# Two feed-forward stages of a two-layer trunk: first weights loaded by SyncE, first product in free PSUM banks, another order of the first 15 block products and of the work beside them

## The chip, the cores and the metric

The kernel runs on one core of a Trainium2 chip. The time is the device time of one execution in microseconds (us), median over several executions; lower is better. Matrix products run on TensorE (PE in the profile), elementwise work on VectorE (DVE), ScalarE (ACT) and GpSimd (POOL); SyncE (SP) issues most transfers. Each engine works through its own queue in order. PSUM, where PE accumulates, has eight banks of 128 x 512 floats.

## The reference

A sequence of 1024 tokens with 1024 features goes through two residual layers (a gated DeltaNet layer, then chunked attention), each followed by the same feed-forward block, and a last RMSNorm. The change touches the feed-forward blocks:

```python
def conv_ffn(xn, w_up, conv_w, conv_b, w_down):
    h = causal_dwconv(xn @ w_up, conv_w) + conv_b
    gate, val = h[..., :FFN_DIM], h[..., FFN_DIM:]
    return (jax.nn.silu(gate) * val) @ w_down
...
h = h + conv_ffn(rmsnorm(h, f_norm[layer]), f_w_up[layer], f_conv[layer], f_conv_b[layer], f_w_down[layer])
```

FFN_DIM is 2816, which is 22 tiles of 128 channels, once for `gate` and once for `val`. The convolution has three taps along the sequence. All is float32.

## The kernel before, in words

**Products.** Every float32 product is made of three matmuls on rounded operands: a value is cut into a high part (a cast to `fp32r`, mostly on ACT) and a low part (the value minus its high part, on POOL or DVE), and `triple` (lines 1394 to 1397) adds high x high, high x low of the moving operand, and low of the weights x high. A block product has four such triples, so 12 matmuls of 128 x 512. In the profile the weights' parts are called uh and ul (ring "u"), dh and dl (ring "d"), and those of the hidden channels eh and el. The activations' parts are xh and xl.

**The feed-forward stage** is one function, `ffn`, called once per layer (layer 0 at line 1974, layer 1 at line 2484; their PE work begins at 674 us and 1896 us). The up-projection of channel tile 0 is done plainly, in eight block products: two halves of the sequence, gate and val, two halves of the 1024 input features. The tiles 1 to 20 use a seven-product (Strassen-like) scheme: product (j, n) is number n of tile j. It needs sums of blocks of the normed activations (`sums`, `highs`, `lows` for n = 7, 6, 5, 4: four 128 x 512 pieces each) and of the weights (`left_sum`), and its results are put together in `after`: product 1 is copied from PSUM to `keep` by ACT, and product 2 is then added into the same PSUM bank; product 4 is added into the bank of product 7, product 3 into that of product 5. From the finished gate and val of a tile come the three taps each (`taps`: step 0 on ACT, steps 1 and 2 on DVE), `silu` on ACT and the product `gated` on DVE. The down-projection takes pairs of tiles, again by seven products (`second(g, n)`, tiles `pd`), whose PSUM results `drain` copies or adds into `stage`.

**The order is written by hand.** `step` appends one PE block to the list `seq`; I number the blocks of a layer from 0. Blocks 0 to 7 are tile 0. From 8 on come the products, before the change (1,1), (2,1), (1,2), (2,2), (1,7), (1,6), (1,5), (2,7), (1,4), (1,3), (2,6), (2,5), (2,4), (3,1), (2,3), so block 14 is (1,5), 17 is (1,3), 18 is (2,6), 19 is (2,5), 20 is (2,4). Then (3,7) is block 23, and from 24 the `second` blocks of the first pair are interleaved; before the change `second(0,5)` is block 29, (3,4) is 30, `second(0,3)` is 31, (3,3) is 32, (4,1) is 33, `second(0,6)` is 34. `at(i, f, rank)` has the other engines' work `f` put into their queues just before block i, lower ranks first. All this lies in a manual schedule, so each engine's queue has exactly this order.

Operands of a product are made two blocks ahead (lines 1608 to 1616): `left_sum` on DVE, the high part on ACT, the low part on DVE for the blocks before (1,3) and on POOL after.

**The norm in front.** `norm_steps` is a generator that is driven from outside: squares and their sum, `pss` (eight tiny matmuls at L374), root and reciprocal, `psb` (eight small matmuls at L387 that spread the factors), then for each of the eight feature tiles k the scaling (L394, DVE), the high part (L395, ACT) and the low part (L383, DVE or POOL). The second half of the sequence is normed while tile 0's first blocks run: `plain` advances the generator at two places, written as (block, triple), in layer 0 (0, 3) for `pss` and (1, 1) for the rest, in layer 1 (1, 3) and (2, 2). Its last steps on the first half in layer 1 are driven by `tail` (line 2419) in the attention stage.

**Transfers and rooms.** `load` (line 1438) brings 128 x 512 weights. For tile 0 of layer 0 it is issued by POOL, otherwise by SP. `cut0` makes tile 0's operands; for the gate (r = 0) casts and low parts are both on POOL.

**PSUM.** In `ffn` the tag "u" has four one-bank tiles and the tag "d" two two-bank tiles. The tag that is used first gets banks 0 to 3, so "u" does (`pu0` at line 1573). In front of layer 0 the accumulators of the last stage (`acco`) sit in the pool's first three banks; in front of layer 1 they are in the last three, since `pB` is opened before `paccB` (lines 2426, 2427).

## Time and profile before

| | |
|---|---|
| median of 3 runs | 2573.83 us (2572.54 to 2575.7) |
| the profiled execution | 2573.15 us, span of its instructions 2571.4 us |
| PE busy | 2506.2 us, 97% of the span |
| DVE busy | 1824.8 us, 71% |
| ACT busy | 1405.4 us, 55% |
| POOL busy | 1484.8 us, 58% |

A row of the timeline gives the start and the length in us, the engine, the line, the operation, the output and the inputs, shapes, and a count of rows put together; in square brackets is the idle time of that engine before it and what ended it. A row of the windows view gives a stretch, its length, each engine's busy time in it with the count of instructions, and at the end the granted clock of PE (1.00 is full), the share of DMA time and GB/s.

### The profile page before, as it was taken

Reading aid. Unit: us, or ns where it says so; the run is one execution under the profiler, and the core shown is the slowest. Engines: PE = TensorE matmul, PEld = TensorE weight load, DVE = VectorE, ACT = ScalarE, POOL = GpSimd, SP = SyncE. Lnnn points to the kernel's source line nnn. Section 1 sums busy time; section 2 is a strip of 40 time slices with the busy share of each in tenths; the row PEclk is TensorE's granted clock in tenths of the full one; section 3 lists DMA queues with packets and bytes.
Section 4 is the critical chain, followed back from the end, with each engine's and each line's share of the span. In section 5 each row is a group of like instructions: output and inputs, shape, how many; then the busy total and the mean of one; then the engine's idle time right before and its main releaser. Section 6 shows DMA issues by size and latency. Waiting matters only on the chain. (4 is left out here: it accounts for less than half of the span.)

```text
span 2571.4 us, 39303 instructions
## 1 busy us (share of the span) xinstructions
PE 2506.2 (97%) x13957; PEld 2081.7 (81%) x13957; DVE 1824.8 (71%) x2956; ACT 1405.4 (55%) x2704; POOL 1484.8 (58%) x1511
## 2 busy tenths in 40 slices
PE   7999999999999999999999999999999999999998
PEld 5878788888777888888788888888877788888877
DVE  5765775454588888888866666666478788888885
ACT  6444555474456555565545555556455656555653
POOL 3655554245537777777725444445453777777770
PEclk9999999999999999999999999999999999999999
DMA  4534445455326676777841211122332467677785
GB/s 128 138 101 121 119 117 164 130 176 167 112 78 136 143 152 143 155 152 152 185 164 46 61 43 48 53 69 71 128 119 78 135 148 147 146 155 153 155 194 189
DMA packets 317061, 325.93 MB, mean 127 GB/s; under 512 B 32832, under 2 KB 240960, under 8 KB 316864
## 3 DMA queue, kind: packets, MB, share of 16 engines
q1 hardware_dynamic: 285728, 219.33, 28.7%
q0 software_dynamic: 26240, 95.43, 20.7%
q10 hardware_dynamic: 4896, 8.65, 1.0%
q8 instruction: 110, 1.80, 0.3%
q14 instruction: 87, 0.71, 0.1%
HBM read 180.68 MB, written 142.67 MB: 126 GB/s over the span
## 5 line engine op out<-in xcount | busy, mean ns | idle before, releaser
L1362 POOL TENSOR_TENSOR ul<-r,uh 128x512 fp32r<-128x512 f32 x276 | 438.3, 1607 | 276.1 <-ACT uh L1383 261.6
L105 POOL TENSOR_TENSOR wlo<-wraw,whi 128x256 fp32r<-128x256 f32 (+3 forms) x338 | 249.3, 768 | 227.1 <-ACT whi L103 192.4
L120 PE MATMUL acc<-xh,whi 128*128 128x512 f32 x896 | 377.8, 422 | 0.2
L122 PE MATMUL acc<-xh,wlo 128*128 128x512 f32 x896 | 354.9, 396 | 3.2 <-POOL wlo L105 3.2
L121 PE MATMUL acc<-xl,whi 128*128 128x512 f32 x896 | 355.1, 396 | 1.0 <-DVE xl L1102 0.6
L1383 ACT CAST uh<-r 128x512 fp32r<-128x512 f32 x290 | 178.2, 623 | 202.0 <-DVE r L1362 159.0
L1397 PE MATMUL pu<-xh,ul 128*128 128x512 f32 x528 | 207.1, 392 | 3.7 <-POOL ul L1362 3.7
L1395 PE MATMUL pu<-xh,uh 128*128 128x512 f32 x528 | 207.0, 392 | 2.9 <-POOL uh L1383 1.4
L1396 PE MATMUL pu<-xl,uh 128*128 128x512 f32 x528 | 206.5, 391 | 1.0 <-POOL xl L383 1.0
L122 PEld LDWEIGHTS acc<-xh,wlo 128*128 128x128 f32 x896 | 169.7, 189 | 41.4 <-POOL wlo L105 3.9
L1749 ACT COPY stage<-pd 128x1024 f32<-128x1024 f32 x180 | 174.9, 1013 | 50.3 <-PE pd L1397 49.4
L121 PEld LDWEIGHTS acc<-xl,whi 128*128 128x128 f32 x896 | 170.8, 191 | 27.3 <-DVE xl L1102 2.7
L120 PEld LDWEIGHTS acc<-xh,whi 128*128 128x128 f32 x896 | 170.7, 190 | 24.6 <-ACT xh L1101 1.1
L1490 DVE SCALAR_TENSOR_TENSOR gate<-gpre,colt,gate 128x1023 f32<-128x1023 f32 (+2 forms) x92 | 180.0, 1957 | 4.7 <-ACT gate L1487 3.8
L1362 POOL TENSOR_TENSOR dl<-a,dh 128x512 fp32r<-128x512 f32 x90 | 153.8, 1709 | 46.0 <-ACT dh L1383 46.0
L2155 POOL TENSOR_SCALAR sS<-sS,st 128x640 f32<-128x640 f32 (+4 forms) x128 | 85.7, 674 | 163.5 <-DVE st L2153 147.9
L1490 DVE SCALAR_TENSOR_TENSOR val<-vpre,colt,val 128x1023 f32<-128x1023 f32 x88 | 151.9, 1726 | 35.7 <-ACT val L1487 35.5
L2145 DVE CUSTOM_DVE_ANT_0 sS<-sc,bt 128x640 f32<-128x640 f32 (+4 forms) x128 | 84.1, 657 | 123.6 <-PE sc L2141 97.0
L1362 DVE TENSOR_TENSOR r<-r,r 128x512 f32<-128x512 f32 x160 | 126.4, 790 | 31.0 <-POOL ul L1362 29.6
L1397 PEld LDWEIGHTS pu<-xh,ul 128*128 128x128 f32 x528 | 99.5, 188 | 26.7 <-POOL ul L1362 6.2
L2213 ACT CAST pTh<-ptp 128x512 fp32r<-128x512 f32 (+2 forms) x176 | 76.1, 452 | 81.2 <-PE ptp L2200 79.6
L1395 PEld LDWEIGHTS pu<-xh,uh 128*128 128x128 f32 x528 | 99.4, 188 | 24.2 <-POOL uh L1383 1.9
(406 smaller groups left out, 7131.9 us busy)
## 6 DMA issues: line engine op xcount, KB each, us to landing
r<-in_f_w_up_dram SPq DMA_DIRECT2D x172, 256.0 KB, 4.3
d_r<-stage POOLq DMA_DIRECT2D x78, 512.0 KB, 7.7
d_c<-stage POOLq DMA_DIRECT2D x70, 512.0 KB, 7.8
a<-in_f_w_down_dram SPq DMA_DIRECT2D x72, 256.0 KB, 2.8
wraw<-in_a_w_in_dram SPq DMA_DIRECT2D x32, 512.0 KB, 4.7
d_e<-stage POOLq DMA_DIRECT2D x32, 512.0 KB, 8.8
wraw<-in_a_w_out_dram SPq DMA_DIRECT2D x16, 512.0 KB, 4.3
d_r<-h ACTq DMA_DIRECT2D x32, 256.0 KB, 3.4
```

The lines of the kernel that those rows point to most:

```text
L105: nc.gpsimd.tensor_tensor(lo[:, c], raw[:, c], hi[:, c].bitcast(F32), op=ALU.subtract)
L120: mm(ps, hi[:, kw, wcol : wcol + P], rh[k][s], start=st, stop=False)
L121: mm(ps, hi[:, kw, wcol : wcol + P], rl[k][s], start=False, stop=False)
L122: mm(ps, lo[:, kw, wcol : wcol + P], rh[k][s], start=False, stop=sp)
L1362: tt = lambda eng, o, a, b, op: eng.tensor_tensor(o, a, b, op=op)
L1383: copy(hi, src)
L1395: mm(ps, w[0][:, cw], x[0], start=first, stop=False, skip_group_check=True)
L1396: mm(ps, w[0][:, cw], x[1], start=False, stop=False, skip_group_check=True)
L1397: mm(ps, w[1][:, cw], x[0], start=False, stop=last, skip_group_check=True)
L1490: nc.vector.scalar_tensor_tensor(t_[:, a:c1], p_[:, a - step : c1 - step], w[:, 2 - step : 3 - step], t_[:, a:c1], op0=ALU.mult, op1=ALU.add)
L1749: nc.scalar.copy(t_, ps)
L2155: nc.gpsimd.tensor_scalar(S, S, st[:, 3:4], 1.0, op0=ALU.mult, op1=ALU.mult)
```

## The change

- `load`: tile 0 of layer 0 is loaded by SP as all others are.
- PSUM: two unused "d" tiles are taken first, so that "d" has banks 0 to 3 and "u" banks 4 to 7; ahead of layer 1 `paccB` is opened before `pB`, so that there too the accumulators are in the first banks.
- `cut0(0, 0)` is now inside the manual schedule at block 0, rank -1. In layer 1 the norm's last step of the first half (the low part of k = 7) is held back and comes right behind it.
- The norm's second beat in layer 1 is at (2, 0) instead of (2, 2). The low part of k = 6 of the second half goes to POOL.
- The order of the first 15 products; `second(0, 3)` one product later; (3,7) gets its low part on DVE; and the places of taps, silus and products `gated` of tiles 0 to 2, and of `after(1, 2)`.

```diff
         def low(t_, k):
-            eng = (nc.gpsimd if k < 4 else nc.vector) if keep and s == 1 else (nc.vector if k % 2 == 0 else nc.gpsimd)
+            eng = (nc.gpsimd if k in (0, 1, 2, 3, 6) else nc.vector) if keep and s == 1 else (nc.vector if k % 2 == 0 else nc.gpsimd)
...
+        H = {'x': {('s', 7): (5, 1), ('h', 7): (6, 1.5), ('s', 6): (6, 2), ('h', 6): (6, 2.01), ('l', 7): (7, 2), ('l', 6): (8, 2), ('s', 5): (9, 2), ('h', 5): (9, 2.01), ('l', 5): (10, 2.002), ('s', 4): (11, 2), ('h', 4): (11, 2.01), ('l', 4): (12, 2)}, 'xl': {7: (), 6: (), 5: (), 4: ()}, 'beats': ({(0, 3): 1, (1, 1): 20}, {(1, 3): 1, (2, 0): 20}), 'first': [(1, 1), (1, 2), (2, 1), (1, 7), (2, 2), (1, 6), (1, 5), (2, 7), (1, 4), (1, 3), (2, 6), (2, 5), (2, 4), (2, 3), (3, 1)], 'o': (2, 3, 5, 7, 8, 9, 11), 'ops': {(3, 7): (0.5, 1.5, 'v')}, 'conv': {0: {'g0': (11, 0), 'v0': (12, 0), 'v1': (13, 2), 'v2': (13, 2.611), 'g1': (15, 2), 'g2': (15, 2.01), 's': (15, 2.204), 'm': (17, 2)}, 1: {'v0': (18, 2), 'v1': (18, 3.206), 'v2': (19, 2), 'g0': (19, 2.01), 'g1': (20, 2), 'g2': (21, 0.903), 's': (22, 1.6), 'm': (23, 1.3)}, 2: {'v0': (24, 2), 'v1': (24, 2.01), 'v2': (25, 2), 'g0': (26, 1.466), 'g1': (26, 2), 'g2': (27, 2), 's': (28, 1.6), 'm': (29, 1.3)}}, 'gp': {1: (18, 0.411), 2: (22, 3)}}
...
-            (nc.gpsimd if j + layer == 0 else nc.sync).dma_start(out=t_, in_=w_up[k0 * P : (k0 + 4) * P, m * P : (m + 1) * P].rearrange("(k p) m -> p k m", p=P))
+            nc.sync.dma_start(out=t_, in_=w_up[k0 * P : (k0 + 4) * P, m * P : (m + 1) * P].rearrange("(k p) m -> p k m", p=P))
...
         first_ps = {}
+        for _ in range(2):
+            pacc.tile([P, SEQ], F32, name="pu1", tag="d", bufs=2)
...
-                    if (i, k) == ((0, 3), (1, 3))[layer]:
-                        next(tail)
-                    if (i, k) == ((1, 1), (2, 2))[layer]:
-                        for _ in tail:
-                            pass
+                    for _ in range(H["beats"][layer].get((i, k), 0)):
+                        next(tail, None)
...
-        first = [(1, 1), (2, 1), (1, 2), (2, 2), (1, 7), (1, 6), (1, 5), (2, 7), (1, 4), (1, 3), (2, 6), (2, 5), (2, 4), (3, 1), (2, 3)]
+        first = H["first"]
...
-                for n, o in zip(ORDER, (2, 3, 5, 6, 8, 9, 11) if g == 0 else (-2, 0, 2, 4, 6, 8, 10)):
+                for n, o in zip(ORDER, H["o"] if g == 0 else (-2, 0, 2, 4, 6, 8, 10)):
...
-            if i < early:
+            if i < early or (j, n) in H["ops"]:
+                rh, rl, eng = H["ops"].get((j, n), (1, 2.5, "v"))
                 low = []
-                at(i - 2, lambda j=j, n=n, low=low: low.append(operand(j, n, False)), 1)
-                at(i - 2, lambda low=low: low[0](), 2.5)
+                at(i - 2, lambda j=j, n=n, low=low: low.append(operand(j, n, False)), rh)
+                at(i - 2, lambda low=low, eng=eng: low[0](nc.vector if eng == "v" else nc.gpsimd), rl)
...
-        cut0(0, 0)
+        at(0, lambda: [cut0(0, 0), [None for _ in env.pop("x7", ())]], -1)
...
-            0: [(11, (g0,), 0), (12, (v0,), 0), (13, (v1,), 2), (13, (v2,), 2.7), (15, (g1, g2), 2), (16, (silu,), 1.6), (17, (gated,), 2)],
-            1: [(18, (v0, v1), 2), (19, (v2, g0), 2), (20, (g1,), 2), (21, (g2,), 2), (22, (silu,), 1.6), (23, (gated,), 1.3)],
-            2: [(24, (v0, v1), 2), (25, (v2, g0), 2), (26, (g1,), 2), (27, (g2,), 2), (28, (silu,), 1.6), (29, (gated,), 1.3)],
+            j: [(i, (dict(v0=v0, v1=v1, v2=v2, g0=g0, g1=g1, g2=g2, s=silu, m=gated)[f],), r) for f, (i, r) in H["conv"][j].items()]
+            for j in range(3)
...
-        for j, i in ((1, 17), (2, 22)):
-            at(i, lambda j=j: after(j, 2), 3)
+        for j, (i, r) in H["gp"].items():
+            at(i, lambda j=j: after(j, 2), r)
...
         def tail(it):
             for n, _ in enumerate(it):
+                if n == KT + 1:
+                    env["x7"] = it
+                    return
                 yield wv.T + (0.8, 2.2)[n] if n < 2 else wv.T + 1.1
...
+        pacc = ph.enter_context(tc.tile_pool(name="paccB", bufs=1, **PS))
         pB = ph.enter_context(tc.tile_pool(name="pB", bufs=1, **PS))
-        pacc = ph.enter_context(tc.tile_pool(name="paccB", bufs=1, **PS))
```

More of the change, by code (lines that the diff above doesn't have):

```diff
@@ L1428, in lows @@
             for k in range(4):
-                tt(nc.vector, X[n][k][1], place[n](k), X[n][k][0].bitcast(F32), sub)
+                tt(nc.gpsimd if k in H["xl"][n] else nc.vector, X[n][k][1], place[n](k), X[n][k][0].bitcast(F32), sub)
         raw, ops = {}, {}
@@ L1467, in operand @@
                 cut_low(src, *ops[j, n], nc.gpsimd)
-            return lambda: cut_low(src, *ops[j, n], nc.vector)
+            return lambda eng: cut_low(src, *ops[j, n], eng)
         pre, conv_t, hid, keep, bank = {}, {}, {}, {}, {}
@@ L1643, in ffn @@
         X[6], X[5], X[4] = more("t2"), more("t1"), more("t4")
-        for i, f, n, r in (
-            (5, sums, 7, 1), (6, highs, 7, 1.5), (6, sums, 6, 2), (6, highs, 6, 2), (7, lows, 7, 2), (8, lows, 6, 2),
-            (9, sums, 5, 2), (9, highs, 5, 2), (10, lows, 5, 2), (11, sums, 4, 2), (11, highs, 4, 2), (12, lows, 4, 2),
-        ):
-            at(i, lambda f=f, n=n: f(n), r)
+        for (f, n), (i, r) in H["x"].items():
+            at(i, lambda f=dict(s=sums, h=highs, l=lows)[f], n=n: f(n), r)
         for i, q in ((0, (2, 11)), (0, (1, 12)), (1, (2, 12)), (6, (2, 21)), (7, (2, 22)), (14, (3, 11)), (16, (3, 21)), (17, (3, 22)), (18, (3, 12))):
```

## The prediction

> **What bounds the kernel now.** I read the page first, then PE's own timeline at the two places where `ffn` begins, then those of POOL, ACT and DVE there, and last the windows view over the first 130 us of both stages.

> ```profile
> PE 2506.2 (97%) x13957; PEld 2081.7 (81%) x13957; DVE 1824.8 (71%) x2956; ACT 1405.4 (55%) x2704; POOL 1484.8 (58%) x1511
> ...
> r<-in_f_w_up_dram SPq DMA_DIRECT2D x172, 256.0 KB, 4.3
> ```

> PE is the bound; only what PE waits for can be won. Matmuls follow each other at 0.23 us:

> ```profile
> 672.81 0.39 PE L121 MATMUL acco<-xl,whi 128*128 128x512 f32 x1
> 673.04 0.39 PE L122 MATMUL acco<-xh,wlo 128*128 128x512 f32 x1
> 674.30 0.47 PE L1395 MATMUL pu<-xh,uh 128*128 128x512 f32 x1 [0.88 <-DVE h L1263]
> ...
> 676.51 0.50 PE L1397 MATMUL pu<-xh,ul 128*128 128x512 f32 x1 [1.50 <-POOL ul L1362]
> ```

> So a block of 12 takes 2.7 us. A row is drawn 0.39 long though the next follows after 0.23, so a wait is the bracket plus 0.16. These are the first two waits of layer 0: 1.04 for the accumulator's bank (L1263 empties it) and 1.66 for the first low part. In a row of the windows view the first figure behind the last count in brackets is PE's granted clock:

> ```profile
> 677.42:680.83 3.41, 3.41 (x12) 2.77 (x11) 0.00 (x0) 0.28 (x1) 3.19 (x3) 0.50 0.68 191
> 773.00:776.40 3.40, 3.40 (x10) 2.63 (x9) 1.19 (x2) 3.20 (x6) 2.59 (x2) 0.50 0.10 35
> 686.00:719.00 33.00, 32.40 (x143) 26.40 (x141) 32.78 (x52) 22.37 (x37) 4.87 (x4) 1.00 0.00 1
> 1911.00:1945.00 34.00, 31.26 (x133) 24.13 (x132) 33.78 (x53) 21.66 (x36) 3.40 (x3) 1.00 0.04 10
> ```

> Two stretches of 3.4 us right behind waits of layer 0 ran at half clock, which costs half of each, 1.7. And from block 4 to block 14 the second engine is as full as PE: DVE is busy for 32.78 of 33.00 and 33.78 of 34.00 us. There a gain counts only if it lets DVE start earlier.

> **Start of layer 0.** POOL and SP:

> ```profile
> 656.55 71.85 SPq L1441 DMA_DIRECT2D r<-in_f_w_up_dram  x12
> 667.13 3.29 POOL L1441 DMA_DIRECT2D r<-in_f_w_up_dram  x4
> 671.35 0.61 POOL L1383 CAST uh<-r 128x512 fp32r<-128x512 f32 x1 [0.93 <-DMA r<-in_f_w_up_dram]
> 674.45 0.78 POOL L1383 CAST uh<-r 128x512 fp32r<-128x512 f32 x1 [2.49 <-DMA r<-in_f_w_up_dram]
> 675.20 4.18 POOL L1362 TENSOR_TENSOR ul<-r,uh 128x512 fp32r<-128x512 f32 x3
> ```

> POOL issues the four loads only at 667.13, when it is through with the weights of the stage before, and spends 3.29 on them. SP stands at its `ffn` loads by 656.55. All four of tile 0 now pass there ahead of the loads of tile 1, which aren't due before block 6, so that delay costs nothing. With the page's 4.3 for a transfer, even doubled, the first is in by 665. POOL then casts from 667.1 (0.78) and subtracts (4.18 / 3 = 1.39), twice: both low parts are there by 671.5, before the last accumulator matmul at 673.04. With "u" in banks 4 to 7 the first block needs no emptied accumulator, so it starts at 673.3. Gone are 1.04 and 1.66, and with them the reason for the first half-clock stretch, 1.7: 4.4. What is late next is the sum for `pss`, due behind block 0 at 676.0:

> ```profile
> 674.56 0.63 ACT L359 ACTIVATE sq<-h 128x512 f32<-128x512 f32 x1 [5.29 <-DVE h L1263]
> 675.23 1.78 DVE L366 TENSOR_TENSOR nacc<-run,sq 128x512 f32<-128x512 f32 x1 [0.47 <-ACT sq L359]
> ```

> The 1.78 was beside POOL's subtractions; POOL will be nearly idle then, so 0.7 to 1.78, ready at 675.9 to 677.0. I take 0.2 of waiting. DVE's chain hangs on `psb` and moves with it. Term: **-4.2** (bounds -4.4 and -3.3, and +2.9 in the third rival).

> **Start of layer 1.** Here SP loaded already, and POOL's order is the point:

> ```profile
> 1888.47 0.37 SPq L1441 DMA_DIRECT2D r<-in_f_w_up_dram  x1
> 1893.57 1.62 POOL L383 TENSOR_TENSOR xl<-h,xh 128x512 fp32r<-128x512 f32 x1 [3.30 <-ACT xh L395]
> 1895.13 1.17 POOL L1383 CAST uh<-r 128x512 fp32r<-128x512 f32 x1
> 1896.38 1.77 POOL L1362 TENSOR_TENSOR ul<-r,uh 128x512 fp32r<-128x512 f32 x1
> 1898.11 1.07 POOL L1383 CAST uh<-r 128x512 fp32r<-128x512 f32 x1
> 1899.26 3.31 POOL L1362 TENSOR_TENSOR ul<-r,uh 128x512 fp32r<-128x512 f32 x2
> ```

> POOL idles 3.30 for the norm's last high part and then does the low part of k = 7 ahead of the first weights. In the new order the weights go first: landed at about 1888.47 + 4.3 = 1892.8, cast 1.17, low part 1.77: 1895.7, where 1898.15 was the end before. But the k = 7 part (1.62), the second cast (1.07) and its low part (1.65) now follow: 1900.1, instead of 1899.26 + 1.65 = 1900.9. So PE wins 2.4 at block 0 and keeps 0.8 to 1.2 of it through block 1; I take 1.0. `psb` then comes two triples earlier, 6 x 0.23 = 1.4, and DVE's chain with it. PE's waits for POOL's low parts in block 4 (L1396 after L383) then go as well, but those are the same microseconds: PE runs into DVE's full queue by block 14 anyway, so DVE's start is the gain. Term: 1.0 + 1.4 = **-2.4** (from 0, if the loads land late, to -3.5).

> **The low part of k = 6 on POOL.** DVE's rows of the norm in layer 0:

> ```profile
> 687.94 1.77 DVE L383 TENSOR_TENSOR xl<-h,xh 128x512 fp32r<-128x512 f32 x1
> ...
> 692.83 0.69 DVE L383 TENSOR_TENSOR xl<-h,xh 128x512 fp32r<-128x512 f32 x1 [0.16 <-ACT xh L395]
> ```

> The low part between these two goes away, but the last one waited for ACT anyway and can't start earlier: 0, at worst +1.1 if POOL's part slows it as POOL slowed the first here (1.77 against 0.69). [...]

> **The new order of products.** (1,2) now follows (1,1) at once and adds into its bank, which ACT must first have copied:

> ```profile
> 703.91 0.39 PE L1397 MATMUL pu<-xh,ul 128*128 128x512 f32 x1
> ...
> 704.33 0.59 ACT L1524 COPY keep<-pu 128x512 f32<-128x512 f32 x1 [1.61 <-PE pu L1397]
> ```

> From 703.91 + 0.23 to 704.92 and a hand-over: a new wait of 0.8 in both layers at block 9. Its cover is that DVE decides block 14 (all its low parts and sums up to there are the same ones as before). Cover gone, it costs 1.6 in all; I take 0.

> **Blocks 17 to 20.** ACT's queue in layer 0, and PE's waits:

> ```profile
> 725.58 3.51 DVE L1490 SCALAR_TENSOR_TENSOR gate<-gpre,colt,gate 128x1023 f32<-128x1023 f32 x2
> 729.80 0.62 ACT L1383 CAST uh<-r 128x512 fp32r<-128x512 f32 x1 [3.40 <-DVE r L1362]
> 730.43 1.28 ACT L1493 ACT_TABLE_LOAD   x1
> 731.73 1.06 ACT L1493 ACTIVATE gate<-gate 128x1024 f32<-128x1024 f32 x1
> 732.70 0.60 ACT L1383 CAST uh<-r 128x512 fp32r<-128x512 f32 x1
> 728.06 0.50 PE L1397 MATMUL pu<-xh,ul 128*128 128x512 f32 x1 [0.54 <-POOL ul L1362]
> 732.07 0.51 PE L1397 MATMUL pu<-xt2h,ul 128*128 128x512 f32 x1 [0.88 <-POOL ul L1362]
> 735.25 0.50 PE L1397 MATMUL pu<-xt1h,ul 128*128 128x512 f32 x1
> 739.01 0.47 PE L1395 MATMUL pu<-xt4h,uh 128*128 128x512 f32 x1 [1.19 <-DVE keep L1362]
> ```

> PE waits 0.70, 1.04, about 0.3 and 1.35 here. `silu(0)` stood behind the high part of (2,6) and delayed that of (2,5), `val`'s first tap and so DVE's `keep`. Now it stands before: the table load falls into ACT's 3.40 of idling, silu runs from 729.1 (the taps' end) to 730.2, the high part of (2,6) ends at 730.8 instead of 730.4, that of (2,5) at 731.4 instead of 733.3. So the second wait grows by 0.4 and the last two, 1.65, go; the first stays. Term: -1.25 per layer, **-2.5** (0 to -6.8, which is all four waits in both layers).

> **`second(0,3)` one product later.** It adds into the banks of `second(0,5)`, which ACT must have copied:

> ```profile
> 771.29 1.93 ACT L1749 COPY stage<-pd 128x1024 f32<-128x1024 f32 x2
> 772.36 0.50 PE L1395 MATMUL pd<-eh,dh 128*128 128x512 f32 x1 [2.87 <-ACT stage L1749]
> 1995.18 0.50 PE L1395 MATMUL pd<-dh,eh 128*128 128x512 f32 x1 [2.15 <-ACT stage L1749]
> ```

> Waits of 3.03 and 2.31, in layer 0 with the second half-clock stretch (1.7): 7.0 together. A product of 2.7 now lies in front of the block, which covers all but 0.3, in layer 0 alone. What is late next is `second(0,6)`, with one product instead of two behind `second(0,3)`: the two copies take 1.93 of that 2.7, which leaves some 0.5 for ACT's queue. I take 0.4 of waits left at both, and 0.4 for (2,3), whose low part and bank are now due one block earlier. Terms: **-7.0** and **+0.8** (bounds: none of it, -7.0).

> Sum: -4.2 - 2.4 - 2.5 - 7.0 + 0.8 = -15.3. Behind both starts PE's rhythm carries the shift to the end. The profiled execution took 2573.15, so 2557.9; the median of the runs is 0.7 above it: **2558.5**.

> **Rivals.** A difference under 0.2%, 5.1 us, can't be told from no change here.

> First: behind block 14 nothing is won. DVE stays full, silu's delay of (2,6) eats the rest, the wait at `second(0,3)` moves to `second(0,6)`, and both waits at block 9 cost 0.8. For it speaks DVE's 99% of busy time; against it that ACT and POOL aren't full (22.37 and 4.87 of the 33.00) and that ACT's 3.40 of idling at blocks 15 to 18 takes up the table load. -4.2 - 2.4 + 1.6 = -5.0: 2568.8. Chance 0.12.

> Second: the half-clock stretches don't go, they move. The wait of 2.31 in layer 1 was followed by no such stretch, so it is not the wait alone that decides. Two such stretches elsewhere: +3.4, 2561.9. Chance 0.15. [...]

> Third: the change doesn't do what it says, since SP gets the rooms of tile 0 only when the last accumulator product has read its weights, 673.04. Then the first low part is there at 673.04 + 4.3 + 0.7 + 1.4 = 679.4, 2.9 later than 676.51: -15.3 + 4.2 + 2.9 = -8.2, 2565.6. POOL's loads at 667.13 without a wait speak against it. Chance 0.05.

> Fourth, slower: the exchanged PSUM pools cost in the attention stage between the layers, which this change touches in nothing else.

> ```profile
> L2145 DVE CUSTOM_DVE_ANT_0 sS<-sc,bt 128x640 f32<-128x640 f32 (+4 forms) x128 | 84.1, 657 | 123.6 <-PE sc L2141 97.0
> ```

> Its 128 score tiles lie in other banks now. If each then cost PE's path 0.15 (a new wait between scores and accumulators), that is +19.2 and 2577.7; from 0.12 each the gain is gone. No row shows a bank's number to matter. Chance 0.03.

> **How the numbers follow.** The forecast has 0.65. The range takes in the second and third rival, up to 2566.0, and below the forecast the unknown ends of two terms (-3.5 for -2.4, half of the further 4.3 at blocks 17 to 20, some luck with the clock): 2552.5. Faster by over 0.2% is forecast, second and third rival and a little of the first: 0.88. Same: most of the first, 0.08. Slower: 0.04.

> **What would show it.** In the changed profile the first `pu` row of layer 0 must follow the last `acco` row after 0.2 to 0.4 us and its L1397 without a bracket; no stretch at 0.50 there. In layer 1 `psb` must come some 2.4 sooner behind the last `acco`. ACT_TABLE_LOAD must stand before the taps' end, the rows at blocks 19 and 20 without brackets, and `second(0,3)` behind (3,3) with no wait for `stage`. A bracket at block 9 from `keep` must appear. The prediction is wrong if DVE's full stretch ends no earlier against PE, or if a wait of over 2 us stands at `second(0,6)`.

## The result

| | before | after |
|---|---|---|
| median of the runs beside each other (6 each) | 2573.07 us | 2556.55 us |
| lowest to highest | 2569.8 to 2575.7 | 2554.21 to 2559.87 |
| ratio, 95% interval | | 0.9938 (0.9927 to 0.9949) |
| profiled execution: time, span | 2573.15, 2571.4 | 2556.85, 2555.1 |

The change makes the kernel 0.62% faster. The page of the changed kernel's profile shows the same work with 5 us less of PE (rows: engine, busy time, share of the span, instructions):

```profile
span 2555.1 us, 39295 instructions
PE 2501.0 (98%) x13957; PEld 2080.8 (81%) x13957; DVE 1827.9 (72%) x2956; ACT 1407.1 (55%) x2704; POOL 1489.0 (58%) x1507
```

To see where the time went I measured, in both traces, the distance between the same PE instructions in each layer (us; start of one to start of the next; "psb" is the norm's second short product, (1,4) is block 16, (2,4) block 20, and (3,4) and (4,4) are the products around `second(0,3)`):

| stretch of the FFN | layer 0 before | after | layer 1 before | after |
|---|---|---|---|---|
| last acco to psb | 9.74 | 5.38 | 11.81 | 11.67 |
| psb to (1,4) | 41.34 | 41.34 | 41.33 | 42.05 |
| (1,4) to (3,4) | 42.48 | 42.90 | 42.48 | 43.01 |
| (3,4) to (4,4) | 39.31 | 35.48 | 36.88 | 33.26 |
| sum | 132.87 | 125.10 | 132.50 | 129.99 |

Only 10.3 of the 16.3 us arise here; 4.2 are there before the first acco of the whole kernel (568.24 against 564.00), in code that the change doesn't touch. A further 2.4 lie between the end of layer 0's rows and the start of layer 1's, where the kernel before has one more stretch at half clock, and 0.6 are lost behind layer 1's. And where blocks 17 to 20 should have won, both layers lost. So the total agreed with the forecast while its parts, at first sight, did not.

The start of layer 0 came as forecast. PE's timeline of the changed kernel, the last accumulator product and what follows (start, duration):

```profile
668.80 0.39 PE L122 MATMUL acco<-xh,wlo 128*128 128x512 f32 x1
669.03 0.39 PE L1396 MATMUL pu<-xh,uh 128*128 128x512 f32 x1
...
669.48 0.39 PE L1398 MATMUL pu<-xh,ul 128*128 128x512 f32 x1
...
671.83 0.35 PE L374 MATMUL pss<-ones,nacc 128*128 128x2 f32 x2
```

No row has a bracket: the first product follows after 0.23, its low part is there, and so is the sum for pss. In blocks 17 to 20 the same view has two waits with a bracket, and the second, at block 18, is 1.9 where it was 1.04:

```profile
719.33 0.50 PE L1398 MATMUL pu<-xh,ul 128*128 128x512 f32 x1 [0.44 <-POOL ul L1362]
724.47 0.50 PE L1398 MATMUL pu<-xt2h,ul 128*128 128x512 f32 x1 [1.73 <-POOL ul L1362]
```

ACT, DVE and POOL of the changed kernel at that place:

```profile
717.68 1.28 ACT L1494 ACT_TABLE_LOAD   x1
720.38 1.06 ACT L1494 ACTIVATE gate<-gate 128x1024 f32<-128x1024 f32 x1 [1.42 <-DVE gate L1491]
721.35 0.60 ACT L1384 CAST uh<-r 128x512 fp32r<-128x512 f32 x1
722.08 1.21 DVE L1362 TENSOR_TENSOR val<-val,gate 128x1024 f32<-128x1024 f32 x1
722.08 5.80 POOL L1362 TENSOR_TENSOR ul<-r,uh 128x512 fp32r<-128x512 f32 x3 [2.81 <-DMA r<-in_f_w_up_dram]
```

The first of the three POOL operations in the last row, by itself:

```profile
722.08 2.33 POOL L1362 TENSOR_TENSOR ul<-r,uh 128x512 fp32r<-128x512 f32 x1 [2.81 <-DMA r<-in_f_w_up_dram]
```

The table load did fall into ACT's idle time and silu(0) starts when the taps end. But its early end lets DVE's gated(0) start at 722.08, in the same moment as POOL's low part of (2,6). DVE takes its 1.21; the low part, for which PE waits, is ready only at 724.4. That is 2.33 us where POOL's low part before it took 1.53 and the one behind it 1.29. And behind that wait the clock drops (windows view; the first figure behind the last count is the granted clock):

```profile
721.92:725.33 3.41, 1.60 (x7) 1.01 (x7) 2.24 (x4) 2.80 (x5) 3.25 (x2) 1.00 0.81 278
725.33:728.74 3.41, 3.41 (x10) 2.64 (x9) 1.69 (x2) 0.00 (x0) 2.55 (x2) 0.50 0.03 10
```

### The profile page after: what moved, and what is told of

Same layout as the page of the kernel before. It is cut to its first block, busy times and chain, and to the rows that moved or that the text cites. A ratio compares the mean times of both kernels' runs of the same rounds, so it can differ in the third digit from the quotient of the medians.

```text
span 2555.1 us, 39295 instructions
## 1 busy us (share of the span) xinstructions
PE 2501.0 (98%) x13957; PEld 2080.8 (81%) x13957; DVE 1827.9 (72%) x2956; ACT 1407.1 (55%) x2704; POOL 1489.0 (58%) x1507
## 5 line engine op out<-in xcount | busy, mean ns | idle before, releaser
L1362 POOL TENSOR_TENSOR ul<-r,uh 128x512 fp32r<-128x512 f32 x274 | 440.2, 1626 | 272.0 <-ACT uh L1384 258.4
L122 PE MATMUL acc<-xh,wlo 128*128 128x512 f32 x896 | 353.0, 394 | 3.2 <-POOL wlo L105 3.2
L121 PE MATMUL acc<-xl,whi 128*128 128x512 f32 x896 | 353.6, 395 | 1.0 <-DVE xl L1102 0.6
L1396 PE MATMUL pu<-xh,uh 128*128 128x512 f32 x528 | 207.0, 392 | 1.4 <-ACT keep L1525 1.4
L1397 PE MATMUL pu<-xl,uh 128*128 128x512 f32 x528 | 206.2, 390 | 0.0
L122 PEld LDWEIGHTS acc<-xh,wlo 128*128 128x128 f32 x896 | 168.9, 188 | 41.5 <-POOL wlo L105 3.9
L121 PEld LDWEIGHTS acc<-xl,whi 128*128 128x128 f32 x896 | 170.1, 190 | 27.1 <-DVE xl L1102 2.5
L1362 POOL TENSOR_TENSOR dl<-a,dh 128x512 fp32r<-128x512 f32 x90 | 154.0, 1711 | 42.3 <-ACT dh L1384 39.1
L1362 DVE TENSOR_TENSOR r<-r,r 128x512 f32<-128x512 f32 x160 | 127.2, 795 | 31.0 <-POOL ul L1362 29.7
L1396 PEld LDWEIGHTS pu<-xh,uh 128*128 128x128 f32 x528 | 99.7, 189 | 22.5 <-ACT keep L1525 2.2
## 6 DMA issues: line engine op xcount, KB each, us to landing
r<-in_f_w_up_dram SPq DMA_DIRECT2D x176, 256.0 KB, 4.2
a<-in_f_w_down_dram SPq DMA_DIRECT2D x72, 256.0 KB, 2.8
d_r<-h ACTq DMA_DIRECT2D x32, 256.0 KB, 3.2
```

What stands on the lines that cost most here:

```text
L121: mm(ps, hi[:, kw, wcol : wcol + P], rl[k][s], start=False, stop=False)
L122: mm(ps, lo[:, kw, wcol : wcol + P], rh[k][s], start=False, stop=sp)
L1362: tt = lambda eng, o, a, b, op: eng.tensor_tensor(o, a, b, op=op)
L1396: mm(ps, w[0][:, cw], x[0], start=first, stop=False, skip_group_check=True)
L1397: mm(ps, w[0][:, cw], x[1], start=False, stop=False, skip_group_check=True)
```

## The experiments

The runs were made in four groups, each on another chip and beside executions of the kernel before (13, 21, 15 and 9 of them); its medians there are 2570.35 to 2570.61, so that the groups can be held against each other. The changed kernel took 2556.03 in one of them. Times are medians; ratios are to the kernel before. The tables of places stand in one long line of the kernel, `H`; the cuts show only those of its entries that differ.

**The kernel before once more**, no edit.

> The kernel before, unchanged, profiled once more. Theory: the FFN's anchors (last acco to pss, psb to (1,4), (1,4) to (2,4), (3,4) to (4,4)) come out within 0.3 us of the first profile wherever no half-clock stretch falls between them, and the stretches outside the FFN lie at other places or in another number, so that the 4.2 us by which the changed kernel reached its first acco sooner is nothing but three such stretches less (5.1) that the change didn't cause. Rival: the stretches before the first acco are at the same places again (148, 312 and 503 us) and the first acco starts within 0.5 us of 568.2; then the changed kernel's 4.2 there belong to the change.

One execution, 2576.04. The first acco is at 568.25 and the stretches at half clock at 148, 312, 503, 677, 773, 1370 and 1780 are there again, with two more at 1899.3 and 1998.3. The pieces without a stretch in them come out as before (psb to (1,4) 41.34 in both layers, (1,4) to (3,4) 42.49 and 42.48); the start of layer 1, now with one, takes 2.1 more (13.86 to psb). So the rival seemed to hold. But over all 14 profiles, of kernels that share all code up to that point, the first acco came at 564.00 to 569.37, with one to four such stretches ahead of it, and the changed kernel itself at 564.00 in one execution and 566.71 in another. The 4.2 is neither the change's nor a property of the kernel before: it goes with the stretches ahead of it, three in the kernel before and one in the changed kernel's first profile, and these with where the clock's grid (below) cuts a wait. PE waits 3.3 near 308 us in both first profiles (3.18 and 3.19 in brackets, for POOL's `wlo`). In the kernel before that wait lies in one piece of the grid, 308.78 to 312.19, and a stretch follows; in the changed kernel 308.90 cuts it into 1.7 and 1.7, and the clock stays up.

**Start only**: the kernel before with the changes of the start; against the changed kernel, `first` and the places of taps, silus and `gated` are as before as well as:

```diff
...
-'o': (2, 3, 5, 7, 8, 9, 11), 'ops': {(3, 7): (0.5, 1.5, 'v')}
+'o': (2, 3, 5, 6, 8, 9, 11), 'ops': {}
...
-0: {'g0': (11, 0), 'v0': (12, 0), 'v1': (13, 2), 'v2': (13, 2.611), 'g1': (15, 2), 'g2': (15, 2.01), 's': (15, 2.204), 'm': (17, 2)}
+0: {'g0': (11, 0), 'v0': (12, 0), 'v1': (13, 2), 'v2': (13, 2.7), 'g1': (15, 2), 'g2': (15, 2), 's': (16, 1.6), 'm': (17, 2)}
...
```

> The kernel before with only the changes at the start: SyncE's loads, the free banks, POOL's new order, the earlier sum for psb, the low part of k = 6. Theory (the terms are separate, and layer 1 gains nothing at its start since nacc is late there): -4.1 in layer 0 and 0 in layer 1, 2569.0, at most 1.7 to either side by one stretch of half clock. Rival 1 (the forecast's terms): -4.2 and -2.4, 2566.5. Rival 2 (the exchanged PSUM pools also win in unchanged stages what the changed profile gained ahead of the first acco, 4.2): 2564.8.

2563.43 (9 runs), 7.0 less; ratio 0.9974 (0.9964 to 0.9984). The forecast's 6.6 fits best, but the interval, some 4 to 9 us, takes in all three cases. Last acco to psb in layer 0 is 5.38 here too. My later theory, that layer 1 gains nothing, is weakened: from the last acco to (1,4) layer 1 takes 52.69 with a stretch at half clock in it, where the kernel before took 53.14 without one.

**Orders only**: the changed kernel with the start as before. Behind the cut, `tail` holds nothing back and the two PSUM pools stand in their old order.

```diff
-            eng = (nc.gpsimd if k in (0, 1, 2, 3, 6) else nc.vector) if keep and s == 1 else (nc.vector if k % 2 == 0 else nc.gpsimd)
+            eng = (nc.gpsimd if k < 4 else nc.vector) if keep and s == 1 else (nc.vector if k % 2 == 0 else nc.gpsimd)
...
-{(1, 3): 1, (2, 0): 20}
+{(1, 3): 1, (2, 2): 20}
...
-            nc.sync.dma_start(out=t_, in_=w_up[k0 * P : (k0 + 4) * P, m * P : (m + 1) * P].rearrange("(k p) m -> p k m", p=P))
+            (nc.gpsimd if j + layer == 0 else nc.sync).dma_start(out=t_, in_=w_up[k0 * P : (k0 + 4) * P, m * P : (m + 1) * P].rearrange("(k p) m -> p k m", p=P))
...
-        for _ in range(2):
-            pacc.tile([P, SEQ], F32, name="pu1", tag="d", bufs=2)
...
-        at(0, lambda: [cut0(0, 0), [None for _ in env.pop("x7", ())]], -1)
+        cut0(0, 0)
...
```

> The changed kernel with the start as before (GpSimd loads tile 0, the first product in the old banks, the old POOL order, the old place of the sum, the low part of k = 6 on DVE); the new order of products, sums, taps and silus and second(0,3) one product later are kept. Theory: -8 at second(0,3) and from -2 to +2 at blocks 17 to 20, 2565 to 2562 with the middle at 2564.5; second(0,3) without a wait in both layers, the wait of 2.1 at block 18 for ul in both layers still there. Rival 1 (forecast's terms for these parts, -2.5 and -6.2): 2564.4 with block 18's wait at 1.4. Rival 2 (the wait at block 18 comes from the new start, since POOL's and DVE's chains are shifted against each other by it): block 18 waits 1.4 or less here, and the time is below 2562.

2561.04 (5 runs), 9.4 less; ratio 0.9967 (0.9955 to 0.9980). With start only this adds up to 16.4, and the whole change took 16.5 in the first runs and 14.4 in the experiments: no large part of the gain hangs on both halves together, but with these intervals a few us of it could. Block 18 waits here as long as in the changed kernel, so its wait comes from the new orders and not from the start. But the clock stayed up behind it in layer 0 (PE's row, then windows):

```profile
730.93 0.50 PE L1398 MATMUL pu<-xt2h,ul 128*128 128x512 f32 x1 [1.72 <-POOL ul L1362]
```

```profile
726.42:729.83 3.41, 2.70 (x11) 1.56 (x9) 3.41 (x6) 2.69 (x5) 1.27 (x1) 1.00 0.76 223
729.83:733.24 3.41, 2.31 (x10) 1.93 (x11) 2.21 (x2) 1.66 (x2) 3.41 (x3) 1.00 0.47 164
733.24:736.65 3.41, 3.41 (x17) 2.83 (x16) 3.08 (x4) 0.99 (x2) 1.41 (x2) 1.00 0.00 0
```

The same wait of 1.9 is cut in two by 729.83, a point of this execution's grid; in the changed kernel's profile it lay in one piece of the grid.

**silu(0) back** behind the high part of (2,6):

```diff
-'s': (15, 2.204), 'm': (17, 2)
+'s': (16, 1.6), 'm': (17, 2)
```

> The changed kernel with silu(0) behind the high part of (2,6), as in the kernel before. Theory (the early silu wins nothing, because gated(0) then starts together with POOL's low part of (2,6) and slows it): gated(0) starts some 1.6 us later, the low part of (2,6) is back to 1.4 to 1.8 us, block 18 waits 1.0 instead of 2.1, but the waits of block 19 and 20 (0.3 and 1.35) come back: 2556.6 plus 0 to 1. Rival 1 (the forecast: silu early wins 1.25 per layer): 2559.1. Rival 2 (the early silu costs, by the half-clock stretch that follows block 18's long wait, 1.7 per layer): 2553.2 and no stretch at blocks 18 to 20.

2557.92 (5 runs), 1.9 more than the changed kernel; ratio 0.9958 (0.9944 to 0.9971), so the two can't be told apart by time alone. In the trace (1,4) to (3,4) takes 42.96 and 43.13, where the changed orders take 41.30 and 41.46 in an execution without a stretch there (POOL's old order, below). gated(0) moves to 726.91, the low part of (2,6) takes 1.46 again and block 18 waits 1.0, but the waits at blocks 19 (0.3) and 20 (1.3) are back, and one of 0.7 comes at (3,7), for its low part from DVE. My theory that the early silu wins nothing fell: it wins 1.7 per layer and gives it back only where a stretch follows.

**The changed kernel once more**, no edit.

> The changed kernel once more, unchanged, as the measure for the runs beside it. Theory of the clock (from six profiles: half-clock stretches lie on a grid of 3.41 us, and one follows whenever PE issued nothing for 2.09 us or more of the grid's stretch before): the waits of 2.1 us at block 18 are followed by a stretch at half clock in four executions of ten each, the wait of 2.4 to 2.8 at layer 1's pss in six of ten; 2553 to 2558 by how many of them hit, and in this profile each stretch again follows 2.09 us or more of idle PE in the grid's stretch before. Rival (stretches come at fixed places of a kernel): both block 18s and layer 1's pss are followed by one again.

2556.03 (5 runs), ratio 0.9947 (0.9934 to 0.9961). Block 18 was followed by a stretch in layer 0 (727.5) and not in layer 1, pss in layer 1 by one instead of two. That is the theory's picture; (1,4) to (3,4) is 42.89 and 41.48.

**second(0,3) alone**: the kernel before with

```diff
-                for n, o in zip(ORDER, (2, 3, 5, 6, 8, 9, 11) if g == 0 else (-2, 0, 2, 4, 6, 8, 10)):
+                for n, o in zip(ORDER, (2, 3, 5, 7, 8, 9, 11) if g == 0 else (-2, 0, 2, 4, 6, 8, 10)):
```

> The kernel before with one change alone: second(0,3) stands one product later. Theory (the wait of 3.03 and 2.31 is the copies of second(0,5), and nothing takes its place): from (3,4) to (4,4) 3.6 us less in each layer, no wait at second(0,3) and under 0.4 at second(0,6), and the half-clock stretch behind layer 0's wait gone: 7.0 to 7.5 less than the kernel before. Rival (the wait moves): 0.5 to 2 at second(0,6) or at the next products, 2 to 4 less.

2566.45 (11 runs), 3.95 less; ratio 0.9987 (0.9978 to 0.9996). The rival holds: the wait for `stage` goes, but others come at the product now in front of it, (3,3), and behind it (PE):

```profile
769.38 0.50 PE L1397 MATMUL pu<-xh,ul 128*128 128x512 f32 x1 [0.78 <-POOL ul L1362]
780.91 0.50 PE L1397 MATMUL pu<-x7h,ul 128*128 128x512 f32 x1 [0.36 <-POOL ul L1362]
784.38 0.50 PE L1396 MATMUL pd<-el,dh 128*128 128x512 f32 x1 [0.68 <-POOL el L1362]
```

(3,4) to (4,4) takes 37.77 and 35.63; with all the new orders (orders only) it is 35.50 and 33.27. The 2.3 between them belong to what is moved beside it. DVE's rows show one such piece: two taps of tile 2, here and then with all the new orders:

```profile
761.47 4.20 DVE L1490 SCALAR_TENSOR_TENSOR gate<-gpre,colt,gate 128x1023 f32<-128x1023 f32 x2
```

```profile
758.11 2.59 DVE L1491 SCALAR_TENSOR_TENSOR gate<-gpre,colt,gate 128x1023 f32<-128x1023 f32 x2
```

At their new places they take 1.6 less, and the sum of weights that stands behind them on DVE, from which ACT cuts the high part of (3,3), comes sooner. Which of the moves (taps of tile 2, the low part of (3,7) on DVE) gives how much of the 2.3 wasn't separated.

**A silu of one column ahead**, so that the table is loaded at block 14 and silu(0) can stand behind the high part of (2,6):

```diff
+    silu_warm = const.tile([P, 1], F32, name="silu_warm")
...
-'s': (15, 2.204), 'm': (17, 2)
+'s': (16, 1.6), 'm': (17, 2)
+        at(14, lambda: nc.scalar.activation(silu_warm, epst, AF.Silu), 2)
```

> The changed kernel with the activation table loaded at block 14 by a silu of one column on another tile, and silu(0) itself behind the high part of (2,6). Theory (the gain at blocks 17 to 20 is the table load taken out of ACT's queue; the early silu(0) costs 0.4 at the high part of (2,6), and gated(0) beside POOL's low part the rest of block 18's wait): the high part of (2,6) starts 0.4 sooner, its low part takes 1.5 instead of 2.3, block 18 waits about 0.9 instead of 2.1, blocks 19 and 20 stay without a wait: 1.2 less per layer, and no half-clock stretch there, which is worth another 0.7 per layer on average: 2552.5 to 2554, 2.5 to 4 less than the changed kernel. Rival 1 (the wait at block 18 is POOL's load by the weights' arrival, not DVE's gated): the wait stays at 1.7 or more, and the time is the changed kernel's. Rival 2 (the early silu itself, by its early gated(0), lets blocks 19 and 20 run): the waits of 0.5 and 1.5 at blocks 19 and 20 come back, 1 to 2 more than the changed kernel.

2568.94 (11 runs), ratio 0.9999 (0.9991 to 1.0008): the gain of the change is gone. Block 18 waits 0.7 in layer 0 and 1.0 in layer 1, and 19 and 20 don't wait, as the theory has it, but the products of the whole FFN are slower: between 830 and 1258 us matmuls that don't wait follow each other at 0.2322 on average instead of 0.2269. None of my three cases had this. The edit did something else as well: in the program as it is built, the new tile moves about half of the other SBUF tiles by 32 bytes, those that are placed behind it from the same side. Two runs settle it. First the same without a new tile,

```diff
+        at(14, lambda: nc.scalar.activation(rsn[:, 0, 0:1], epst, AF.Silu), 2)
```

> The silu_warm kernel without its new tile: the silu of one column that loads the table writes a column of rsn, which is idle then, so that every tile lies where it lies in the changed kernel. Theory (the 13 us that silu_warm lost came from the tile: all tiles behind it lay 32 bytes further on, and each FFN product then followed the last after 0.2322 instead of 0.2269): the pitch is 0.2269 again, block 18 waits about 0.9, blocks 19 and 20 don't wait: 2552.5 to 2554.5, 2 to 3.5 less than the changed kernel. Rival (the early table load or the moved silu slows the FFN): 2568 to 2570 again.

2554.71 (5 runs), ratio 0.9940 (0.9927 to 0.9952). Then the changed kernel with nothing but an unused tile:

```diff
+    const.tile([P, 1], F32, name="pad")
```

> The changed kernel with a tile of one column that nothing uses, so that all tiles allocated later lie 32 bytes further on; no instruction differs. Theory (the place of the tiles sets the pitch): FFN products at 0.2322, 2569 to 2571, 13 to 15 more than the changed kernel. Rival (the silu of the other kernel was the cause): 2556.

2570.33 (10 runs), ratio 1.0002 (0.9993 to 1.0012). Windows of 50 us in the middle of the FFN, the changed kernel and then this one (PE's busy time and matmuls are the first pair):

```profile
1050.00:1100.00 50.00, 49.87 (x221) 40.92 (x220) 41.81 (x38) 28.88 (x41) 38.77 (x30) 1.00 0.76 155
```

```profile
1050.00:1100.00 50.00, 50.00 (x217) 40.39 (x216) 39.22 (x39) 29.63 (x43) 38.47 (x31) 1.00 0.69 148
```

217 matmuls for 221 at full clock and almost without a wait: the unused tile alone is worth 14 us here. The change itself moves no SBUF tile in the built programs, and the pitch is 0.2269 in the kernel before too, so this has no part in its gain. The early table load with silu(0) behind wins a little: (1,4) to (3,4) takes 40.82 and 40.91.

**POOL's old order at the start of layer 1**, the norm's low part ahead of the first weights:

```diff
-        at(0, lambda: [cut0(0, 0), [None for _ in env.pop("x7", ())]], -1)
+        def start0():
+            if layer == 0:
+                cut0(0, 0)
+            for _ in env.pop("x7", ()):
+                pass
+            if layer == 1:
+                cut0(0, 0)
+
+        at(0, start0, -1)
```

> The changed kernel with POOL's old order at the start of layer 1: the norm's last low part ahead of the first weights' high and low part. Theory (DVE's sum nacc, not POOL's first low part, sets the start of layer 1, and POOL's earlier subtractions slow DVE's additions): block 0 waits 2 to 2.5 again for its first low part, the sum is ready 7 to 8 us behind the last acco instead of 8.76, and from there to psb the time is the same within 0.6 us as in the changed kernel, so the whole time is too. Rival 1 (the forecast: the order wins 1.0): 1.0 more than the changed kernel. Rival 2 (the contention alone counts): the sum and all behind it come 1.5 sooner, 1.5 less.

2555.87 (5 runs), ratio 0.9947 (0.9934 to 0.9961): as the changed kernel, to 0.2 us. The changed kernel first (PE, DVE, POOL; the last acco is at 1880.11):

```profile
1888.92 1.57 PE L374 MATMUL pss<-ones,nacc 128*128 128x2 f32 x8 [2.45 <-DVE nacc L369]
1878.63 1.68 DVE L383 TENSOR_TENSOR xl<-h,xh 128x512 fp32r<-128x512 f32 x1
1880.23 1.78 DVE L361 TENSOR_TENSOR nacc<-nacc,spare 128x512 f32<-128x512 f32 x1
...
1887.30 1.57 DVE L369 TENSOR_TENSOR nacc<-nacc,spare 128x512 f32<-128x512 f32 x1
1878.46 1.30 POOL L1362 TENSOR_TENSOR ul<-r,uh 128x512 fp32r<-128x512 f32 x1
1879.71 1.75 POOL L383 TENSOR_TENSOR xl<-h,xh 128x512 fp32r<-128x512 f32 x1
```

and with POOL's old order (the last acco is at 1881.99):

```profile
1883.83 0.50 PE L1396 MATMUL pu<-xh,uh 128*128 128x512 f32 x1 [1.45 <-POOL uh L1384]
1885.68 0.50 PE L1398 MATMUL pu<-xh,ul 128*128 128x512 f32 x1 [1.12 <-POOL ul L1362]
1890.81 0.95 PE L374 MATMUL pss<-ones,nacc 128*128 128x2 f32 x8
1880.22 0.68 DVE L383 TENSOR_TENSOR xl<-h,xh 128x512 fp32r<-128x512 f32 x1
1880.83 0.68 DVE L361 TENSOR_TENSOR nacc<-nacc,spare 128x512 f32<-128x512 f32 x1
...
1887.30 1.59 DVE L369 TENSOR_TENSOR nacc<-nacc,spare 128x512 f32<-128x512 f32 x1
```

In the old order PE waits at block 0 (1.6 and 1.3) and comes to pss 8.82 behind the last acco, when the sum has long been ready (1888.89, 6.9 behind). In the new one PE runs through block 0, but POOL's subtractions, now earlier, run beside DVE's additions and stretch them from 0.68 to 1.7; the sum is ready only 8.76 behind the last acco, and PE waits there. 8.81 or 8.82: the wait changes its place.

**gated(0) late**, one step behind POOL's low part:

```diff
-'m': (17, 2)
+'m': (18, 1.5)
```

> The changed kernel with gated(0) one step later, behind POOL's low part of (2,6). Theory (DVE's gated and POOL's low part, both reading two inputs from SBUF, slow each other): that low part takes 1.5 instead of 2.3, block 18 waits 1.3 instead of 2.1, which is under the 2.09 of idle PE that brought a half-clock stretch, and nothing later waits for the product that gated makes: 0.8 less per layer and 0.7 more on average for the stretches, 2553 to 2555. Rival 1 (the low part is long whoever runs beside it): 2556. Rival 2 (the later gated delays DVE's keep and val): block 20 or (2,3) waits 0.5 to 1, 2556 to 2558.

2554.83 (5 runs), ratio 0.9938 (0.9926 to 0.9951). DVE, POOL and PE:

```profile
725.06 1.77 DVE L1362 TENSOR_TENSOR val<-val,gate 128x1024 f32<-128x1024 f32 x1
724.47 5.75 POOL L1362 TENSOR_TENSOR ul<-r,uh 128x512 fp32r<-128x512 f32 x3 [2.81 <-DMA r<-in_f_w_up_dram]
725.80 0.50 PE L1398 MATMUL pu<-xt2h,ul 128*128 128x512 f32 x1 [0.68 <-POOL ul L1362]
```

Now POOL starts first: PE has its low part 1.33 after POOL's start instead of 2.39, and gated takes 1.77 instead of 1.21, which nobody waits for. Block 18's wait falls from 1.9 to 0.84, no stretch follows, and (1,4) to (3,4) takes 40.87 and 40.94.

**Three of these together**: the silu of one column into rsn, gated(0) late, POOL's old order in layer 1.

> The changed kernel with the three edits that cost nothing together: the table loaded ahead by a silu of one column into rsn, silu(0) behind the high part of (2,6), gated(0) one step later still, and POOL's old order at the start of layer 1. Theory (the single gains are block 18's: a wait of 0.7 instead of 2.1 and no half-clock stretch behind it): (1,4) to (3,4) takes 40.5 to 41.0 in both layers, where the changed kernel takes 41.3 or with a stretch 42.9; the whole time 2553 to 2555, 1 to 3 less than the changed kernel. Rival (gated later than POOL's low part delays val's taps): (2,4) or (2,3) waits and (1,4) to (3,4) takes 41.3 or more: 2556.

2551.83 (5 runs, 18.5 less than the kernel before; ratio 0.9929, 0.9915 to 0.9943), the fastest here, though its interval still overlaps the changed kernel's. (1,4) to (3,4) takes 40.77 and 40.88, and the profile has no stretch at half clock in either start or at block 18.

## Why the prediction was right, point by point

Terms are compared by the rows of the first table, where I can in executions in which no stretch at half clock fell into the row. Layer 0 of the kernel before has one at its start and one at second(0,3) in both of its profiles, so there it is in the figures.

- **Start of layer 0**: -4.2 forecast, 9.74 to 5.38 = -4.4. Right in each step: loads and banks both, and the sum for pss is in time.
- **Start of layer 1**: -2.4 forecast, of it 1.0 for POOL's order and 1.4 for psb two triples earlier. From the last acco to (1,4) the old start takes 53.1 (before) and 53.5 (orders only), the new one 51.8 (silu back), and the new one with POOL's old order 51.7 (POOL's old order; 51.75 combined): the 1.4 came, the 1.0 didn't. (The first pair of profiles doesn't show the forecast's sign, psb 2.4 sooner: 11.81 and 11.67, as two stretches fell into the changed kernel's.) The step that failed is the one that took the 1.0 as won at block 1: what it left out is that POOL's earlier subtractions lengthen DVE's sum, which PE meets a block later. With the new POOL order six of eight executions also had a stretch at half clock behind that wait; the changed kernel's own two took 53.7 and 52.8. With the old one it was one of six, and that one took 55.2 (before once more).
- **Low part of k = 6, the wait at block 9**: 0 forecast. Block 9 waits 0.83 for `keep` in both layers, and psb to (1,4) is 41.34 before and after in layer 0: DVE decides, the cover holds. DVE's last low part starts 10.05 behind psb before and 10.06 after, so POOL's part there cost nothing.
- **Blocks 17 to 20**: -1.25 per layer forecast, 42.48 to 41.30 and 41.46 = -1.1. The size is right, the way isn't. The wait at block 18 grew by 0.9 and not by 0.4, since gated(0) came beside POOL's low part; that at block 20 went, and 0.4 more is won at the next products. And I missed what the longer wait does to the clock: 1.6 lost (42.90 for 41.30) in four of eight passes: both layers of the changed kernel's first profile, layer 0 of its second, layer 1 of orders only, and none of the other four. On average over the eight the row takes 42.2, a gain of 0.3 and not 1.25.
- **second(0,3)**: -7.0 and +0.8 forecast, 7.4 measured in the first pair of profiles. The working failed: one product in front of the block doesn't do it. By itself it brings 1.5 in layer 0 (39.31 to 37.77) and 1.25 in layer 1 (36.88 to 35.63), because (3,3) then waits for its low part; 2.3 more per layer come from the moves beside it, which the prediction didn't price. So that the size came near the forecast's 6.2 is luck. The 0.8 for new waits at `second(0,6)` and (2,3) didn't come either: neither waits in the changed kernel. And the stretch at half clock isn't worth 1.7 in layer 1: in the kernel before the same piece takes 36.88 without and 37.09 with one, as the waits that follow are then shorter. In layer 0 all three profiles with the old place have a stretch there, so what it costs isn't shown.
- **Sum**: -4.4 - 1.4 - 2.2 - 7.4 = -15.4, forecast -15.3; by medians -16.5 with the result and -14.4 in the experiments. The -1.4 and -2.2 are those of executions without a stretch in the row; by the shares above, some 2 of them are lost on average (an estimate). That the first pair of profiles gives -16.3 is luck: 4.2 came ahead of the first acco, with two stretches fewer there, and about as much was lost to the stretches at both block 18s and at layer 1's pss. To that extent the second rival came true as well.
- The first, third and fourth rival fell: much is won behind block 14, SP has its rooms in time, and the attention stage takes the same time (first to last score tile 449.5 before, with two stretches at half clock in it, 447.9 after, with one, and 447.9 with the old pools and one stretch in orders only).

## What to carry to other kernels

When a wait goes, look for the next releaser on the engine that was moved forward, and for an engine whose operations take longer beside it: here POOL's earlier work lengthened DVE's additions from 0.68 to 1.7, and an early DVE product lengthened POOL's low part from 1.28 to 2.33. See to it that the operands of what takes a moved block's place are early too: `second(0,3)` alone brought 1.5 and 1.25, with the moves beside it 3.8 and 3.6. And compare kernels stage by stage in executions whose clock dips lie alike, with new tiles placed so that the old ones don't move: here the dips moved the first acco by up to 5.4 us, and one unused tile was worth 14.

## What the runs showed of the hardware

**DVE beside POOL.** When gated(0) starts some 0.01 ahead of POOL's low part, as it does in both layers of the changed kernel, gated takes 1.21 and the low part 2.33. With gated ahead by 0.55 it is 1.23 and 1.83 (silu back), with POOL ahead by 0.59 it is 1.77 and 1.28 (gated late). In these three the one that started first kept its length (1.21, 1.23 and 1.28), and the other took 0.5 to 1.1 longer. DVE's and POOL's rows of silu back, then POOL's of gated late:

```profile
726.91 1.23 DVE L1362 TENSOR_TENSOR val<-val,gate 128x1024 f32<-128x1024 f32 x1 [1.94 <-ACT gate L1494]
727.47 1.83 POOL L1362 TENSOR_TENSOR ul<-r,uh 128x512 fp32r<-128x512 f32 x1 [1.36 <-DMA a<-in_f_w_down_dram]
```

```profile
724.47 1.28 POOL L1362 TENSOR_TENSOR ul<-r,uh 128x512 fp32r<-128x512 f32 x1 [2.81 <-DMA r<-in_f_w_up_dram]
```

**The place of tiles.** One unused tile of 4 bytes in each partition slows the FFN's matmuls from 0.2269 to 0.2322. In another stage it doesn't: in the stretch from 1500 to 1740 us the pitch is 0.230 without and with it. In the built programs the activations' parts xh and xl move by 32 bytes, while the weights' parts (uh, ul, dh, dl) and those of the hidden channels (eh, el) stay. But the down-projection's products, which read only tiles that stay, are slowed too, from 0.2269 to 0.2300 (the up-projection's to 0.2334). So the place of a matmul's own operands can't be the whole cause; what is stays open.
